# DeltaNet's substitution on VectorE: a reordered mixer in a two-layer kernel on Trainium2

## The chip, the cores and the metric

The kernel runs on one core of one Trainium2 chip. Its engines work side by side, each through its own list of instructions in order: TensorE (PE in the profile) multiplies, VectorE (DVE) and GpSimd (POOL) do elementwise work, ScalarE (ACT) evaluates functions and copies, and SyncE (SP) issues the transfers. An instruction starts when the one ahead of it on its engine is done and the semaphores that it waits for have been raised. The metric is the device time of one execution in microseconds (us), the median of several runs.

## What is computed

Two layers of a backbone run on 384 tokens (128 of a prompt, 256 of a sample) of 1024 features, in float32. Layer 0 mixes the tokens with two recurrences, HGRN2 and a gated DeltaNet, each with four heads and in both directions; layer 1 mixes them with neighbourhood attention; an MLP ends each layer. Only layer 0's mixer is touched. Of the reference that is:

```python
q_a, f_fw, f_bw, i_a, g_a, qkv_b, g_b, a_fw, a_bw, b_fw, b_bw = _split(h @ w_in, _AB_SIZES)
qa = _heads(jax.nn.silu(q_a), H_A) * DK_A ** -0.5
va = _heads(i_a, H_A)
...
qkv = jax.nn.silu(_short_conv(qkv_b, conv_w))
...
# DeltaNet, per chunk of CHUNK tokens and direction:
L = jnp.where(tri, jnp.exp(jnp.where(tri, diff, 0.0)), 0.0)
kb = k * beta[..., None]
A = jnp.where(strict, jnp.einsum('bhntd,bhnsd->bhnts', kb, k) * L, 0.0)
T = jnp.eye(CHUNK) + A
u = triangular_solve(T, v * beta[..., None], lower=True, unit_diagonal=True)
w = triangular_solve(T, kb * jnp.exp(g)[..., None], lower=True, unit_diagonal=True)
```

The shifts, scales and gates of every sub-layer (the modulation) are products of a condition vector with a 1024 x 6144 matrix per layer.

## The kernel before

**Projections.** A weight block of 256 columns arrives in two loads (`raw`, L204, three buffers). ScalarE rounds each to its high half (`whi`, L209), and VectorE, or GpSimd for the blocks named in `ON_POOL`, subtracts to get the low half (`wlo`, L210). Three products of rounded numbers then stand for one in float32. `fm_block` (L645 to L647) makes a block with features on the partitions, 48 matmuls of 384 columns; `tm_half` (L687 to L689) makes the values with tokens on the partitions, 72 matmuls of 256 columns. In the step table f0 to f3 are HGRN's forget gates, q0 and q1 its queries, v0 and v1 its values, c0 to c5 blocks of DeltaNet's queries, keys and values ahead of the convolution (c2 and c3, the keys, are done first, in the part ahead of the table), g0 to g3 output gates, and m the normalised outputs turned into the out-projection's input.

**Evacuations.** `evac_f` (L714, L715) and `evac_q` (L705, L706) make gates and queries, with a sigmoid on ScalarE and an operation on VectorE. `evac_conv` copies a block to `cr` and convolves it on VectorE (L933, L935), and GpSimd multiplies by the sigmoid (L943, L944) ahead of PE's transposes (L949).

**DeltaNet.** A tile is 128 tokens, that is four chunks of 32; there are three tiles, two directions and four heads, 24 matrices of 128 x 128. `gdn_prep` makes the decay `L` (POOL L996) and multiplies the key products by it (L997), and copies each matrix's four diagonal blocks of 32 x 32 to `hyB` (L1000). `gdn_solve` transposes and weights these blocks, sends them through device memory (`s1`, L1038, L1039) so that each of 96 partitions gets one 32 x 32 system (L1043), and inverts all of them by forward substitution: 31 steps of two dependent operations on GpSimd (L1052, L1053). The result goes back through `s2` (L1055, L1057). `gdn_levels` builds inverses of 64 and 128 from them (L1086 and following), with an evacuation times the weights `cd` after each product (L1091, L1120); `gdn_step` runs the recurrence over the tiles.

**HGRN.** `hgrn_tile` multiplies queries by decays (L746, L747), makes the attention's diagonal blocks (PE L745, DVE L748), and then climbs the levels (PE L757, L762; DVE L769, L771, L780).

**Modulation.** `ada_rest` makes what the later sub-layers need, in 12 steps; a step loads two pieces of the matrix (`adr`, two buffers, L323 and L362) and multiplies each by the conditions (PE L326, L367).

**The order.** The table `STEPS` says in which order the parts are written: a letter with a number for a block, h, d and a for some steps of HGRN, DeltaNet and modulation. A scheduler orders each engine's instructions ahead of time, by a simulated timeline with the written order as its priority; on the chip the order is fixed. A table of pairs (`ORDER`) adds constraints: an instruction written inside `behind("x")` is placed no earlier than those marked by the names listed for x. On SP the loads stand in one list with the solve's transfers.

```python
STEPS = """
d f3 f1 f2 d q1 a2 q0 d h a2 h a h c4 h a d h3 d c5 h a2 d h v0 h d h d v1 a d h3
c0 h3 c1 h5 d2 h d2 h d h7 g0 g1 d m g2 g3 a3
"""
ON_POOL = {1: (0, 1), "c5": (0,), "q0": (0,)}
```

## Time and profile before

| | us |
|---|---|
| median of 3 runs | 1136.76 |
| lowest and highest run | 1135.27, 1770.32 |
| the profiled execution | 1139.19 |
| its span in the profile | 1137.3 |
| start: norm, first modulation, first projections (0 to 57) | 57.0 |
| the rest of layer 0's projections and the mixer (57 to 322.6) | 265.6 |
| out-projection, MLP of layer 0, layer 1 (from 322.6) | 814.7 |
| PE busy from 131.0 to 322.6 | 177.3 of 191.6 |

The span is what the profiler saw between the first and the last instruction; the device time of the same execution is 1.9 us longer. The stages are windows of the span: the out-projection's first product begins at 322.58. Rows of a view name the line of the kernel, the engine, the operation, what is written and read (buffer numbers left out), and the shape as partitions x elements.

### The profile page before, as it was taken

Reading aid. Unit: us, or ns where it says so; the run is one execution under the profiler, and the core shown is the slowest. Engines: PE = TensorE matmul, PEld = TensorE weight load, DVE = VectorE, ACT = ScalarE, POOL = GpSimd, SP = SyncE. Lnnn points to the kernel's source line nnn. Section 1 sums busy time; section 2 is a strip of 40 time slices with the busy share of each in tenths; the row PEclk is TensorE's granted clock in tenths of the full one; section 3 lists DMA queues with packets and bytes.
Section 4 is the critical chain, followed back from the end, with each engine's and each line's share of the span. In section 5 each row is a group of like instructions: output and inputs, shape, how many; then the busy total and the mean of one; then the engine's idle time right before and its main releaser. Section 6 shows DMA issues by size and latency. Waiting matters only on the chain.

```text
span 1137.3 us, 17975 instructions
## 1 busy us (share of the span) xinstructions
PE 1081.7 (95%) x6853; PEld 937.8 (82%) x6853; DVE 762.3 (67%) x1188; ACT 485.1 (43%) x874; POOL 277.2 (24%) x295
## 2 busy tenths in 40 slices
PE   6989969999998999999999999999988999999998
PEld 3868857988986898888889788888668889998987
DVE  3678499995467698968887654878748773333333
ACT  4464333342445543433334444656636433333330
POOL 0054894231204011111112252324012011111102
PEclk9989989999998999999999999999989999999999
DMA  8953725333162687766674147566425764433301
GB/s 290 292 168 107 220 79 162 129 108 110 38 218 78 244 275 261 260 202 222 226 248 134 41 101 211 153 185 167 119 74 184 281 203 130 133 126 126 99 38 56
DMA packets 142091, 184.66 MB, mean 162 GB/s; under 512 B 36803, under 2 KB 113685, under 8 KB 142005
## 3 DMA queue, kind: packets, MB, share of 16 engines
q1 hardware_dynamic: 141685, 183.44, 51.0%
q8 instruction: 54, 0.88, 0.3%
q14 instruction: 32, 0.26, 0.1%
q10 hardware_dynamic: 320, 0.07, 0.0%
HBM read 171.53 MB, written 4.61 MB: 155 GB/s over the span
## 4 chain that ended last, share of the span: by engine, by line
PE 74%; DVE 7%; DMA 6%; POOL 6%; issue 2%; SPq 2%; ACT 2%; POOLq 0%; DVEq 0%; ACTq 0%
PE acc L1340 7%; PE acc L1341 7%; PE acc L1342 7%; PE tmp L1355 7%; PE tmp L1356 7%; PE tmp L1354 7%; POOL sm L1053 2%; POOL sm L1052 2%; PE po L1731 2%; DMA ada<-in_ada_w 2%; PE acc L646 2%; PE acc L645 2%; PE acc L647 1%; PE acc L672 1%; PE acc L673 1%
## 5 line engine op out<-in xcount | busy, mean ns | idle before, releaser
L210 DVE TENSOR_TENSOR wlo<-raw,whi 128x1024 fp32r<-128x1024 f32 x192 | 238.0, 1250 | 167.2 <-ACT whi L209 145.5
L209 ACT ACTIVATE whi<-raw 128x1024 fp32r<-128x1024 f32 x198 | 205.9, 1050 | 335.0 <-PE acc L1342 190.6
L1374 POOL TENSOR_TENSOR h<-h 128x384 f32<-128x384 f32 x56 | 69.5, 1242 | 424.9 <-ACT h L1371 423.7
L1341 PE MATMUL acc<-wlo,h 128*128 128x512 f32 x380 | 148.5, 391 | 0.1
L1340 PE MATMUL acc<-whi,h 128*128 128x512 f32 x380 | 146.0, 393 | 0.6 <-issue 0.6
L346 DVE SCALAR_TENSOR_TENSOR adc<-adr,scz,adc 128x1024 f32<-128x1024 f32 x98 | 128.5, 1342 | 10.3 <-DMA adr<-in_ada_w 10.1
L1342 PE MATMUL acc<-whi,h 128*128 128x512 f32 x380 | 121.2, 391 | 0.0
L1340 PEld LDWEIGHTS acc<-whi,h 128*128 128x128 f32 x380 | 71.2, 188 | 20.6 <-ACT whi L209 5.0
L1355 PE MATMUL tmp<-hyA,whi 128*128 128x384 f32 (+1 forms) x256 | 85.1, 333 | 2.2 <-DVE hyA L565 2.2
L1354 PE MATMUL tmp<-hyA,whi 128*128 128x384 f32 (+1 forms) x256 | 84.1, 334 | 3.0 <-DVE hyA L564 3.0
L1354 PE MATMUL tmp<-hyB,whi 128*128 128x384 f32 (+1 forms) x256 | 83.8, 329 | 1.2 <-DVE hyB L564 1.2
L1356 PE MATMUL tmp<-hyA,wlo 128*128 128x384 f32 (+1 forms) x256 | 84.8, 332 | 0.0
L1355 PE MATMUL tmp<-hyB,whi 128*128 128x384 f32 (+1 forms) x256 | 84.0, 329 | 0.7 <-DVE hyB L565 0.7
L1341 PEld LDWEIGHTS acc<-wlo,h 128*128 128x128 f32 x380 | 71.4, 188 | 14.3 <-DVE wlo L210 0.5
L1342 PEld LDWEIGHTS acc<-whi,h 128*128 128x128 f32 x380 | 71.0, 188 | 13.7
L1356 PE MATMUL tmp<-hyB,wlo 128*128 128x384 f32 (+1 forms) x256 | 82.1, 328 | 0.0
L645 PE MATMUL acc<-hyA,whi 128*128 128x384 f32 x208 | 74.1, 356 | 0.0
L646 PE MATMUL acc<-hyA,whi 128*128 128x384 f32 x208 | 71.4, 343 | 0.0
L647 PE MATMUL acc<-hyA,wlo 128*128 128x384 f32 x208 | 71.0, 342 | 0.0
L1375 DVE TENSOR_TENSOR h<-h,h 128x384 fp32r<-128x384 f32 (+2 forms) x72 | 37.8, 526 | 40.6 <-POOL h L1374 39.8
L1354 PEld LDWEIGHTS tmp<-hyA,whi 128*128 128x128 f32 x256 | 48.7, 191 | 4.4 <-ACT km L560 3.4
L1355 PEld LDWEIGHTS tmp<-hyA,whi 128*128 128x128 f32 x256 | 49.3, 192 | 3.3 <-DVE hyA L565 2.4
(454 smaller groups left out, 2357.7 us busy)
## 6 DMA issues: line engine op xcount, KB each, us to landing
raw<-in_w_mlp SPq DMA_DIRECT2D x128, 512.0 KB, 3.8
adr<-in_ada_w SPq DMA_DIRECT2D x80, 512.0 KB, 4.7
raw<-in_w_in_ab SPq DMA_DIRECT2D x34, 512.0 KB, 4.7
ada<-in_ada_w SPq DMA_DIRECT2D x32, 256.0 KB, 5.5
raw<-in_w_qkv_na SPq DMA_DIRECT2D x32, 256.0 KB, 3.8
raw<-in_w_out_ab SPq DMA_DIRECT2D x8, 512.0 KB, 4.5
m<-gs SPq DMA_DIRECT2D x8, 512.0 KB
raw<-in_w_qkv_na SPq DMA_DIRECT2D x8, 512.0 KB
```

The lines of the kernel that those rows point to most:

```text
L209: self.nc.scalar.activation(hi, x, AF.Copy)
L210: (eng or self.nc.vector).tensor_tensor(lo, x, hi.bitcast(F32), op=ALU.subtract)
L346: nc.vector.scalar_tensor_tensor(acc[v], raw, s[v], acc[v], op0=ALU.mult, op1=ALU.add)
L645: nc.tensor.matmul(pg[n], whi(k)[:, c], hhi[:, k], start=(k == 0), stop=False)
L646: nc.tensor.matmul(pg[n], whi(k)[:, c], hlo[:, k], start=False, stop=False)
L647: nc.tensor.matmul(pg[n], wlo(k)[:, c], hhi[:, k], start=False, stop=(k == KT - 1))
L1340: nc.tensor.matmul(pg, shi, w2hi(n)[:, o], start=start, stop=False)
L1341: nc.tensor.matmul(pg, shi, w2lo(n)[:, o], start=False, stop=False)
L1342: nc.tensor.matmul(pg, slo, w2hi(n)[:, o], start=False, stop=last)
L1354: nc.tensor.matmul(pg[n], w1hi(k)[:, c], hhi[:, k, tc_], start=(k == 0), stop=False)
L1355: nc.tensor.matmul(pg[n], w1hi(k)[:, c], hlo[:, k, tc_], start=False, stop=False)
L1356: nc.tensor.matmul(pg[n], w1lo(k)[:, c], hhi[:, k, tc_], start=False, stop=(k == KT - 1))
```

## The change

The substitution goes to VectorE. The 48 systems of one direction lie in partitions 0 to 47 and those of the other in 64 to 111. The diagonal blocks are no longer copied and transposed on the chip: four transfers write them from the matrices to `s1` in pieces of 128 bytes, eight bring them to the partitions; two copies that reverse the order of 48 x 1024 elements stand for the transposition of one direction. After the solve eight transfers write `s2`, four write the inverses straight into the diagonal blocks of the matrices, one brings the other form, which is transposed once. The weights `cd` are multiplied into the matrices when they are made (`weigh`, four operations of 128 x 128 for each), so the levels' evacuations become plain copies on ScalarE; the other scales are renamed to match.

ScalarE also takes the second operation of `evac_f`, a copy in `evac_q` and the convolution's first tap; GpSimd takes the multiplication in `evac_q` and the low halves of v0 and v1, one half of q1 and of c4, and no longer one of c5. The queries' and values' blocks are all written ahead of HGRN's and DeltaNet's steps. HGRN's steps are placed behind the solve, the transposition of its result behind HGRN's query products, some memsets of GpSimd late, and each modulation step marked "!" behind the block ahead of it.

```diff
+    ("step", "!"): ["block"],
+    "hgrn": ["solve"],
+    "solved": ["hq"],
+    "zero": ["q", "lo"],
...
 STEPS = """
-d f3 f1 f2 d q1 a2 q0 d h a2 h a h c4 h a d h3 d c5 h a2 d h v0 h d h d v1 a d h3
-c0 h3 c1 h5 d2 h d2 h d h7 g0 g1 d m g2 g3 a3
+f3 a! f1 f2 a! q1 a! q0 a! v0 a! v1 h3 d2! a! d c4 h a! d h c5 h a! d h3 d h d h a! d2 h3
+c0 a! h3 c1 a! h5 d2 h d2 h d a! h7 g0 g1 d m g2 g3
 """
-ON_POOL = {1: (0, 1), "c5": (0,), "q0": (0,)}
+ON_POOL = {1: (0, 1), "q1": (0,), "q0": (0,), "v0": (0, 1), "v1": (0, 1), "c4": (0,)}
...
-            nc.vector.tensor_mul(self.qa[:, :, h], s, pv)
+            nc.scalar.activation(self.qa[:, :, h], pv, AF.Copy)
+            self.mark["q"] = nc.gpsimd.tensor_tensor(self.qa[:, :, h], self.qa[:, :, h], s, op=ALU.mult)
...
-            nc.vector.tensor_scalar(self.G[:, :, d, h], s, self.lb1[:, h:h + 1], self.lb[:, h:h + 1],
-                                    op0=ALU.mult, op1=ALU.add)
+            nc.scalar.activation(self.G[:, :, d, h], s, AF.Identity, scale=self.lb1[:, h:h + 1], bias=self.lb[:, h:h + 1])
...
-            nc.vector.tensor_scalar(acc, raw[:, 0:386], w(0), None, op0=ALU.mult)
+            nc.scalar.activation(acc, raw[:, 0:386], AF.Copy, scale=w(0))
...
-                nc.vector.tensor_mul(self.NT_[:, t, d], pk, L)
-                for b in range(4):
-                    r = slice(32 * b, 32 * b + 32)
-                    nc.vector.tensor_copy(self.NC[r, d, t], self.NT_[r, t, d, :, r])
+                self.weigh(self.NT_[:, t, d], pk, L, t, d)
+
+    def weigh(self, out, pk, L, t, d):
+        for h in range(4):
+            self.nc.vector.scalar_tensor_tensor(out[:, h], pk[:, h], self.cd[:, t, d, h:h + 1], L[:, h], op0=ALU.mult, op1=ALU.mult)
...
+        for b in range(4):
+            nc.sync.dma_start(s1[rows(b)], self.diagonal(b))
+        for d, x in enumerate((A0, A)):
+            for b in range(4):
+                nc.sync.dma_start(x[part(b, d)], blocks(s1, b, d))
...
+        reverse(A, A0)
+        e, n = nc.vector, 112
         for j in range(31):
             m, w = 31 - j, j + 1
...
+            e.tensor_tensor(t, A[:n, w:, j:j + 1].broadcast_to([n, m, w]), X[:n, j:j + 1, :w].broadcast_to([n, m, w]), op=ALU.mult)
+            self.mark["solve"] = e.tensor_tensor(X[:n, w:, :w], X[:n, w:, :w], t, op=ALU.subtract)
+        reverse(A0, X)
...
+        for d, x in enumerate((A0, X)):
+            for b in range(4):
+                nc.sync.dma_start(blocks(s2, b, d), x[part(b, d)])
+        nc.sync.dma_start(XC, s2)
         for b in range(4):
+            nc.sync.dma_start(self.diagonal(b), s2[rows(b)])
...
-            nc.vector.tensor_mul(pb[T], p[T], cd[T].broadcast_to([32, NT, 4, 32]))
+            nc.scalar.activation(pb[T], p[T], AF.Copy)
...
-            nc.vector.tensor_mul(pb[T, c], p[T, :len(ts)], cd[T, c].broadcast_to([64, len(ts), 4, 64]))
+            nc.scalar.activation(pb[T, c], p[T, :len(ts)], AF.Copy)
...
+        with self.behind("solved"):
+            nc.vector.transpose(self.blocks[:, 1], self.blocks[:, 0])
```

What the scheduler makes of it is seen in each engine's list. First SP, where the results of the solve leave. In the list of before, `sm_139_846` is the solve's result, `s_838` is `s2`, and `raw` and `adr` are weight and modulation loads:

```order
L204 DMA raw_2538<-in_w_in_ab 128x4x256
L362 DMA adr_2283<-in_ada_w 128x1024
L1055 DMA s_838<-sm_139_846 24x32x32 x4
L362 DMA adr_2285<-in_ada_w 128x1024
L388 DMA gs_1936<-ada_1256 2x512 x2
L1057 DMA hyB_645<-s_838 128x768
L204 DMA raw_2540<-in_w_in_ab 128x4x256
```

And of the changed kernel, where `sm_139_826` and `sm_138_825` are the result and its reversed half, `s_832` is `s2`, `m_120_747` the matrices, `raw_1401` belongs to v1, and `raw_1718` and `raw_1720` to c4:

```order
L208 DMA raw_1401<-in_w_in_ab 128x4x256
L208 DMA raw_1718<-in_w_in_ab 128x4x256
L1069 DMA s_832<-sm_139_826 12x32x32 x2
L1069 DMA s_832<-sm_138_825 12x32x32 x4
L1069 DMA s_832<-sm_139_826 12x32x32 x2
L1072 DMA m_120_747<-s_832 32x24x32 x2
L1070 DMA hyB_645<-s_832 128x768
L1072 DMA m_120_747<-s_832 32x24x32 x2
L208 DMA raw_1720<-in_w_in_ab 128x4x256
L329 DMA adr_1391<-in_ada_w 128x1024
L329 DMA adr_1393<-in_ada_w 128x1024
```

The transfers of the solve moved ahead in the list, past ten or more weight loads, and the loads of a fifth modulation step stand behind them.

Second PE, between the values. Before, products of modulation and of HGRN stand among v0's, and loads that came long ahead of the solve's end serve them:

```order
L687 MATMUL acc_2019<-whi_2015,hyA_130 128x256
L326 MATMUL ada_1260<-adr_1926,scz 32x512 x2
L688 MATMUL acc_2019<-whi_2015,hyA_131 128x256
L689 MATMUL acc_2019<-wlo_2016,hyA_130 128x256
L687 MATMUL acc_2019<-whi_2015,hyA_130 128x256
```

In the changed kernel the last products of v0 (`acc_1365`), the fifth modulation step and the first products of v1 (`acc_1411`):

```order
L694 MATMUL acc_1365<-whi_1311,hyA_131 128x256
L695 MATMUL acc_1365<-wlo_1312,hyA_130 128x256
L332 MATMUL ada_994<-adr_1391,scz 32x512 x2
L332 MATMUL ada_994<-adr_1393,scz 32x512 x2
L693 MATMUL acc_1411<-whi_1403,hyA_128 128x256
L694 MATMUL acc_1411<-whi_1403,hyA_129 128x256
```

The values are now whole blocks, and v1 stands behind a modulation step whose loads are those at the end of SP's list above.

Third GpSimd, from the decay's last products on. Before, the steps of the solve begin there, with the products for HGRN's keys (`km`) to follow among them:

```order
L996 TENSOR_TENSOR m_121_750<-m_121_750,tri 128x512 x4
L210 TENSOR_TENSOR wlo_1282<-raw_1277,whi_1281 128x1024
L1046 MEMSET sm_139_846 96x1024
L1047 MEMSET sm_139_846 96x32
L1052 TENSOR_TENSOR sm_140_847<-sm_138_841,sm_139_846 96x31
L1098 MEMSET sm_203_1345 32x12x32
```

In the changed kernel, `wlo_1230` belongs to q0, `wlo_1308` and `wlo_1312` to v0, `wlo_1404` and `wlo_1408` to v1, and L713 are the queries' products:

```order
L214 TENSOR_TENSOR wlo_1230<-raw_1225,whi_1229 128x1024
L745 TENSOR_TENSOR km_1491<-x 128x512
L745 TENSOR_TENSOR km_1514<-x 128x512
L745 TENSOR_TENSOR km_1537<-x 128x512
L214 TENSOR_TENSOR wlo_1308<-raw_1303,whi_1307 128x1024
L214 TENSOR_TENSOR wlo_1312<-raw_1305,whi_1311 128x1024
L713 TENSOR_TENSOR hyB_647<-hyB_647,cv_1209 128x3x128
L713 TENSOR_TENSOR hyB_647<-hyB_647,cv_1213 128x3x128
L214 TENSOR_TENSOR wlo_1404<-raw_1399,whi_1403 128x1024
L713 TENSOR_TENSOR hyB_647<-hyB_647,cv_1287 128x3x128
L214 TENSOR_TENSOR wlo_1408<-raw_1401,whi_1407 128x1024
L713 TENSOR_TENSOR hyB_647<-hyB_647,cv_1291 128x3x128
```

The 62 operations of the solve are gone from GpSimd; on VectorE they now follow one another with a single split (L214) among them, and HGRN's query products (L752, L753) stand right behind.

More of the change, by code (lines that the diff above doesn't have):

```diff
@@ L209, in split @@
         self.nc.scalar.activation(hi, x, AF.Copy)
[L210 removed]
+        ins = (eng or self.nc.vector).tensor_tensor(lo, x, hi.bitcast(F32), op=ALU.subtract)
+        if eng:
+            self.mark["lo"] = ins
     def split_w(self, raws, a, b, ring="", pool=()):
@@ L646, in fm_block @@
                         nc.tensor.matmul(pg[n], whi(k)[:, c], hlo[:, k], start=False, stop=False)
-                        nc.tensor.matmul(pg[n], wlo(k)[:, c], hhi[:, k], start=False, stop=(k == KT - 1))
+                        self.mark["block"] = nc.tensor.matmul(pg[n], wlo(k)[:, c], hhi[:, k], start=False, stop=(k == KT - 1))
         for n in range(2):
@@ L675, in tm_parts, with tm_half @@
         return part
-    def tm_half(self, src, hh, evac):
+    def tm_half(self, src, hh, evac, pool=()):
         nc = self.nc
         hhi, hlo = hh
-        whi, wlo = self.split_w(self.slab(src.rearrange("(k p) n -> p k n", p=P), KT, 256), KT, 256)
+        whi, wlo = self.split_w(self.slab(src.rearrange("(k p) n -> p k n", p=P), KT, 256), KT, 256, pool=pool)
         for t0, n in ((0, 2), (2, 1)):
@@ L688, in tm_half @@
                     nc.tensor.matmul(pg[:, t - t0], hlo[:, k, c], whi(k), start=False, stop=False)
-                    nc.tensor.matmul(pg[:, t - t0], hhi[:, k, c], wlo(k), start=False, stop=(k == KT - 1))
+                    self.mark["block"] = nc.tensor.matmul(pg[:, t - t0], hhi[:, k, c], wlo(k), start=False, stop=(k == KT - 1))
             evac(t0, n, pg)
@@ L794, in hgrn_steps @@
             for x in g:
-                next(x)
+                with self.behind("hgrn"):
+                    next(x)
                 yield
@@ L1022, in gdn_eps, with diagonal @@
         nc.vector.tensor_scalar(self.qe, pq, EPS * EPS * P, None, op0=ALU.add)
+    def diagonal(self, b):
+        r = slice(32 * b, 32 * b + 32)
+        return self.nt[r].rearrange("p d t h c -> p d (t h) c")[:, :, :, r]
     def gdn_solve(self):
         nc = self.nc
-        NC = self.NC
-        f = lambda x: x.rearrange("p d t h c -> p (d t h c)")
-        N2 = self.block(1)
-        nc.vector.transpose(f(N2), f(NC))
-        for d in range(2):
-            nc.vector.tensor_mul(N2[:, d], N2[:, d], self.cd[:, :, d].unsqueeze(3).broadcast_to([P, NT, 4, 32]))
@@ new lines, in gdn_solve @@
+        s1 = self.dp.tile([P, 2, 12, 32], F32, tag="s1", name="s1")
+        s2 = self.dp.tile([P, 2, 12, 32], F32, tag="s2", name="s2")
+        rows = lambda b: slice(32 * b, 32 * b + 32)
+        blocks = lambda s, b, d: s[rows(b), d].rearrange("i m j -> m i j")
+        part = lambda b, d: slice(64 * d + 12 * b, 64 * d + 12 * b + 12)
+        for b in range(4):
+            nc.sync.dma_start(s1[rows(b)], self.diagonal(b))
+        for d, x in enumerate((A0, A)):
+            for b in range(4):
+                nc.sync.dma_start(x[part(b, d)], blocks(s1, b, d))
@@ new lines, in gdn_solve @@
+            self.mark["solve"] = e.tensor_tensor(X[:n, w:, :w], X[:n, w:, :w], t, op=ALU.subtract)
+        reverse(A0, X)
+        XC, XD = (self.blocks[:, j].rearrange("p (d m c) -> p d m c", d=2, c=32) for j in range(2))
+        for d, x in enumerate((A0, X)):
+            for b in range(4):
+                nc.sync.dma_start(blocks(s2, b, d), x[part(b, d)])
+        nc.sync.dma_start(XC, s2)
+        for b in range(4):
+            nc.sync.dma_start(self.diagonal(b), s2[rows(b)])
+        self.Xc = [XD[:, d].rearrange("p (t h) c -> p t h c", t=NT) for d in range(2)]
@@ L1069, in gdn_levels @@
         N = XT = self.NT_
-        cd = self.cd[:, :, d].unsqueeze(3)
         tag = "gd"
-        for b in range(4):
-            r = slice(32 * b, 32 * b + 32)
-            nc.vector.tensor_copy(XT[r, :, d, :, r], self.XTc[d][r])
         first = lambda o, L: slice(o, o + L)
@@ L1097, in gdn_levels @@
         loc = lambda r: slice(r.start - o64, r.stop - o64)
-        nc.gpsimd.memset(X[S, :, :, loc(T)], 0.0)
+        with self.behind("zero"):
+            nc.gpsimd.memset(X[S, :, :, loc(T)], 0.0)
         for r in (S, T):
@@ L1474, in layer0 @@
         for step in STEPS.split():
-            kind, n = step[0], int(step[1:] or 1)
+            kind, n = step[0], int(step[1:].strip("!") or 1)
             if kind in chains:
                 for _ in range(n):
-                    next(chains[kind], None)
+                    with self.behind("step", step[-1]):
+                        next(chains[kind], None)
             elif kind == "f":
```

73 lines of the change are left out of this document (27 added, 46 removed).

## The prediction

> **What bounds the kernel now.** I read the page's engine table and slices first, then the windows over the mixer of layer 0, then what the matmul engine waited for there, then the timelines of the solve.
>
> ```profile
> PE 1081.7 (95%) x6853; PEld 937.8 (82%) x6853; DVE 762.3 (67%) x1188; ACT 485.1 (43%) x874; POOL 277.2 (24%) x295
> 114.00:142.00 28.00, 27.05 (x206) 22.90 (x204) 13.77 (x13) 10.92 (x15) 22.98 (x31) 1.00 0.71 221
> 142.00:171.00 29.00, 20.00 (x311) 17.13 (x310) 28.96 (x34) 9.12 (x15) 27.16 (x27) 0.88 0.26 85
> 131.10:322.60 191.50, 177.22 (x1942) 160.12 (x1941) 152.99 (x245) 71.79 (x156) 79.66 (x90) 0.97 0.36 111
> PE tmp L949 <- POOL cv L943: 5.4, 2, 3.1
> PE hg L757 <- DVE hyB L748: 2.8, 1, 2.8
> PE hg L757 <- DVE hyB L771: 2.4, 2, 1.4
> ```
>
> A window row gives its length, then the busy time of PE, PEld, DVE, ACT and POOL with their counts, the granted clock and the DMA share. TensorE is busy 95% of the span, so a change of the other engines can win only where PE idles or runs slowly, or lose by making PE wait. The changed code lies between about 75 and 322.6 us, where the out-projection begins. From 131.1 on, PE idles 191.5 - 177.2 = 14.3 us; 9.0 of that lies between 142 and 171, where VectorE is busy all the time and GpSimd 27.2 of 29. The waits name the convolution's products on GpSimd, queued behind the solve, and HGRN's levels on VectorE. That idle time, with the slow clock behind it, is what the change can win.
>
> ```profile
> 117.38 0.25 POOL L1052 TENSOR_TENSOR sm<-sm,sm 96x31 f32<-96x31 f32 x1 [5.71 <-DMA sm<-s]
> 180.30 0.58 POOL L1053 TENSOR_TENSOR sm<-sm,sm 96x31 f32<-96x31 f32 x1
> 108.10 0.33 SPq L1039 DMA_DIRECT2D s<-g  x1
> 112.95 2.10 SPq L1043 DMA_DIRECT2D sm<-s  x4
> 180.91 2.06 SPq L1055 DMA_DIRECT2D s<-sm  x4
> 185.59 0.34 SPq L1057 DMA_DIRECT2D hyB<-s  x1
> 131.06 0.62 PE L326 MATMUL ada<-adr,scz 128*32 128x512 f32 x2
> 122.28 0.44 PE L645 MATMUL acc<-hyA,whi 128*128 128x384 f32 x1
> 322.58 0.48 PE L672 MATMUL acc<-whi,hyB 128*128 128x512 f32 x1
> ```
>
> The solve holds GpSimd from 117.4 to 180.9, with other work between. Its results are back after a hop of about 9 us, yet PE has the projections of c4, c5 and the values to do meanwhile, so no wait names the solve itself. A projection block takes 131.06 - 122.28 = 8.8 us. Blocks and modulation steps end at 131.1, and the rest of the mixer takes 191.5 us more.
>
> **The solve on VectorE.** 62 operations of 31 to 256 elements, 10,912 elements in all.
>
> ```profile
> 91.61 0.18 DVE L971 TENSOR_TENSOR cd<-beta,kr 128x24 f32<-128x24 f32 x1
> 117.69 1.23 DVE L210 TENSOR_TENSOR wlo<-raw,whi 128x1024 fp32r<-128x1024 f32 x1 [5.16 <-ACT whi L209]
> L997 DVE TENSOR_TENSOR m<-hg,m 128x512 f32<-128x512 f32 x6 | 4.1, 685 | 0.1
> L1000 DVE COPY hyB<-m 32x128 f32<-32x128 f32 x24 | 7.3, 304 | 0.4
> L1167 DVE SCALAR_TENSOR_TENSOR sm<-sm,eg,gd 128x128 f32<-128x128 f32 x8 | 2.2, 342 | 0.0
> ```
>
> Two rows fix the price: 0.18 us for 24 elements and 1.23 for 1024 make (1.23 - 0.18)/1000 = 1.05 ns an element and 0.155 fixed. A dependent step adds about 0.045 (from L971's start to L972's below it is 0.22 us, against 0.18 busy). So 62 x 0.2 + 10,912 x 1.05 ns = 23.9 us, plus one split of 1.2 that stands in the middle. On GpSimd it was 63.5.
>
> Ahead of it, the 24 weighted products at 0.34 (L1167) replace 6 at 0.69 and 24 copies at 0.30: 8.2 for 11.4 us, and two transposes and two products go. I put the last product at 98. The first hop out stands on SP's queue behind a weight load whose buffer waits for GpSimd's split, so I put its four issues at 99.5 to 101.6. From L1039's issue to the first L1043 passes 4.85 us; eight issues in place of four, 0.52 each by L1043 and L1055, take 4.2, and from the last issue to the first operation 2.3 passed before. The solve starts at 101.1 + 4.85 + 4.2 + 2.3 = about 112, for 117.4.
>
> **Contention.** Beside the solve, GpSimd now has the low halves of v0 and v1 (q0's comes just ahead), three products that make HGRN's keys (`km`), and four query products: about 17 us.
>
> ```profile
> 91.83 1.29 DVE L972 TENSOR_TENSOR cs<-cd,eg 128x24 f32<-128x24 f32 x1
> 91.80 3.74 POOL L996 TENSOR_TENSOR m<-m,tri 128x512 f32<-128x512 f32 x3
> 134.81 3.44 DVE L747 TENSOR_TENSOR hq<-hyB,m 128x512 f32<-128x512 f32 x1
> 135.33 2.38 POOL L210 TENSOR_TENSOR wlo<-raw,whi 128x1024 fp32r<-128x1024 f32 x1
> L944 POOL TENSOR_TENSOR m<-cv,cv 128x256 f32<-128x256 f32 x8 | 7.4, 927 | 0.0
> L739 POOL TENSOR_TENSOR km<-x 128x512 f32<-128x512 f32 x3 | 3.8, 1274 | 0.0
> L769 DVE TENSOR_TENSOR x<-x,m 128x512 f32<-128x512 f32 x21 | 18.2, 878 | 0.1
> ```
>
> The 17 us: four splits at 2.38, three products for keys at 1.27, and four products of 384 elements at about 0.95 (an estimate, near L944's 256 elements and under the 512 of L739) make 17.1. L972, as small as L971, took 1.29 in place of 0.18, as long as one of the GpSimd products beside it; L747 took 3.44, and 2.38 of it lies under one GpSimd split. Against that L769, much of which ran beside GpSimd's small solve steps, is at 0.88 on average, some quarter above the 0.69 that L997 takes for as many. Every operation of the solve waits for the one before it, so a stall cannot be made up. The lower end is 0, the upper 17; the splits are of the form that held up L747 wholly, some of the 17 us may lie ahead of the solve, and I take 10. The solve then ends at Ts = 112 + 23.9 + 1.2 + 10 = 147; by the ends 137 and 154.
> The Trainium skill, page "SBUF — State Buffer", section on who interferes with whom, has a VectorE operation with two SBUF inputs and a GpSimd operation exclude each other for a whole instruction. L972's 1.29 agrees with that, L769's 0.88 less plainly; the fourth rival is this case.
>
> **The queue behind the solve.** On SP, behind the solve's eight writes (L1069 of the new kernel, which wait for its end), the four back into the triangles and the one into `hyB`, now stands the modulation load `adr_1391`. On PE its products stand between v0 and v1, and v1, HGRN and DeltaNet's levels stand behind them.
>
> ```profile
> 115.15 0.98 SPq L323 DMA_DIRECT2D adr<-in_ada_w  x2
> 88.70 0.74 PE L645 MATMUL acc<-hyA,whi 128*128 128x384 f32 x1
> 119.96 1.05 PE L326 MATMUL ada<-adr,scz 128*32 128x512 f32 x4 [0.67 <-DMA adr<-in_ada_w]
> 121.29 1.05 PE L326 MATMUL ada<-adr,scz 128*32 128x512 f32 x4 [0.28 <-DMA adr<-in_ada_w]
> 184.93 0.38 PE L687 MATMUL acc<-whi,hyA 128*128 128x256 f32 x1
> 189.22 0.28 PE L689 MATMUL acc<-wlo,hyA 128*128 128x256 f32 x1
> 78.50:88.90 10.40, 9.76 (x32) 5.39 (x32) 5.37 (x10) 8.33 (x22) 4.48 (x6) 0.58 0.49 168
> 366.00:370.50 4.50, 4.39 (x20) 4.39 (x21) 1.96 (x5) 1.45 (x3) 0.55 (x1) 0.50 0.39 118
> ```
>
> After Ts come eight issues at 0.52 (4.2), their landing (L1055's last issue at about 182.4, L1057 at 185.6 with two other issues between: 2.5), five issues more (1.8) and the two loads' own (0.9): the second load is issued at Ts + 9.4. The rows of `adr` give 119.96 - 115.15 = 4.8 and, for the second, issued some 0.5 later, 5.6; I take 5.0. So the step's products start at Ts + 14.4 = 161.4 and take 1.0.
>
> PE gets there much earlier. f1 starts at 88.7 as before, f1, f2, q1 and q0 take 4 x 8.8, four modulation steps some 1.0 each, and v0 36 matmuls in 4.57 us twice (the two rows of values: 184.93 to 189.50), 9.1: v0 ends at 137. PE stands still for about 24 us; the ends of the stall give 14 to 31. After that v1 takes 9.1, plus a slow clock: the two last rows, windows just behind idle stretches, show 10.4 us at 0.58 and 4.5 us at 0.50, a loss of 4.4 and 2.2; I take 3.
> On this the Trainium skill, page "TensorE: Matmul & The Clock Gate", part 1, has about 3.4 us of half rate after an idle stretch, which would lose 1.7; the two stretches here are longer, and the measurement decides.
>
> **The rest of the mixer.** What PE did after 131.1 was 191.5 us. The values in it go: 144 matmuls at 4.57/36 are 18.3, and 15 of them at half rate 1.4, so 19.7. The same seven modulation steps are left. I drop all 14.3 us of idle time: GpSimd no longer holds the convolution's products back, and HGRN's inputs are done while PE stands. Left: 157.5 (a few us of slow clock stay in it, as an allowance for waits that I cannot see).
>
> End of the mixer: Ts + 14.4 + 1.0 + 9.1 + 3 + 157.5 = Ts + 185.0 = 332, against 322.6: 9.4 us later. Layer 0's MLP and layer 1 are untouched. The span 1137.3 becomes 1146.7; the profiled execution took 1139.19, 2.4 more than the median of 1136.76, so I add the difference to the median: 1146.
>
> **The smaller edits, at nothing.**
>
> ```profile
> L1010 DVE TENSOR_TENSOR m<-gd,m 128x512 f32<-128x512 f32 x6 | 3.8, 683 | 2.6 <-PE gd L1008 2.6
> L1074 DVE COPY m<-hyB 32x384 f32<-32x384 f32 x8 | 4.3, 539 | 0.1
> L1120 DVE TENSOR_TENSOR sm<-gd,cd 64x512 f32<-64x512 f32 (+1 forms) x4 | 2.2, 556 | 2.0 <-PE gd L1118 1.9
> L1091 DVE TENSOR_TENSOR g<-gd,cd 32x384 f32<-32x384 f32 x4 | 2.2, 554 | 0.1
> ```
>
> The two pb evacuations (L1091, L1120) go to ScalarE, 4.4 us off VectorE, and so do the convolution's first tap and evac_f: ScalarE is busy 71.8 of 191.5. The attention's weights cost VectorE 8.2 for 3.8; L1074's eight copies (4.3) go, so VectorE comes out about even and stays below PE: 153.0 less the query products and splits moved ahead or to GpSimd. If that cover fails it is the second rival. HGRN behind the solve, and the memsets late, lie inside PE's stall. Where they lie ahead of f1 they win nothing either: I keep its start at 88.7.
>
> **The rivals.**
> First, no stall: if the load lands before v0 ends (Ts under 122, hence a solve of under 10 us, or another issue order), v1 ends at 137 + 1 + 9.1 = 147.1, the mixer at 304.6, and the time is 1118.8. For it: PE's 14.3 idle us do go and the solve is much shorter. Against it: the queue's order is fixed.
> Second, on the other side: VectorE keeps PE waiting after v1 as it did, because the attention's weights, the levels and HGRN's tiles now fall together with nothing but GpSimd to share them. If PE loses the 14.3 us again, the time is 1146 + 14.3 = 1160.3. For it: VectorE's 28.96 of 29 from 142 to 171, where PE lost 9.0. Against it: GpSimd's solve, which slowed VectorE there, is gone. It decides if VectorE is busy more than 0.97 in the 60 us after v1.
> Third, the change does next to nothing: GpSimd and VectorE interleave, the stall is 0 to 3 us, PE's pause of 14 to 17 us eats the idle time won. Ts = 137 to 140, time 1136 to 1139. L769's row speaks for it, L972's against.
> Fourth, the solve waits out all of GpSimd's 17.1 us, as L747 waited out a split: Ts = 154, and the time is 1146 + 7 = 1153. For it L972 and L747, against it L769.
>
> **How the numbers follow.** Chances: the forecast (1139 to 1151) 0.40, no stall 0.14, VectorE-bound 0.18, next to nothing 0.14, all of the stall 0.14. The predicted time is the forecast's 1146. The range leaves out part of the first rival and the upper part of the second, 0.1 on either side: 1121 to 1160. Beyond 2%, about what a measurement of this kernel can tell from no change, means under 1114 or over 1159.5: faster takes 0.05 (no stall and less slow clock), slower 0.13 (two thirds of the second rival, and a little of the fourth).
>
> **What would show it.** Right: a PE wait of 14 to 31 us for `adr` between v0 and v1, a half-rate clock behind it, the solve from about 112 to 147 with operations of 0.2 to 0.45 us and some stretched to over 1 beside GpSimd's splits, no wait of over 1 us for the convolution's GpSimd products. Wrong: the load issued ahead of the solve's writes, a solve of 25 us beside busy GpSimd, or waits for VectorE of over 10 us after v1.

## The result and the profile after

The changed kernel takes 1148.29 us (median of 4 runs, 1146.67 to 1151.33) for 1136.01 of the kernel before beside it: a ratio of 1.0115 [1.0093, 1.0137]. One of the four runs of the kernel before was a slow one, 1770.32 us, and is not in the ratio; without it that median is 1135.27, and the change is 13.0 us slower. That is clear of the noise (the interval is 0.2% to either side), though under the 2% that the prediction took as the least that can be told. The profiled execution took 1148.93, its span is 1147.2, 9.9 longer than before.

The engine table of the page after the change:

```profile
PE 1073.2 (94%) x6853; PEld 933.8 (81%) x6853; DVE 747.4 (65%) x1214; ACT 500.8 (44%) x906; POOL 251.0 (22%) x243
```

VectorE and GpSimd have less to do and ScalarE more, as the change means it; TensorE stays the engine that sets the time. What PE waited for between 74 us and the out-projection (total, times, longest):

```profile
PE ada L332 <- DMA adr<-in_ada_w: 27.1, 1, 27.1
PE tmp L955 <- ACT cv L960: 4.5, 1, 4.5
```

One wait of 27.1 us stands where many small ones stood; those for the convolution on GpSimd and for the levels on VectorE are gone. Windows over v0, the stall with the modulation step, v1, the rest of the mixer up to the out-projection, and one inside that rest:

```profile
129.76:138.66 8.90, 8.90 (x76) 8.69 (x72) 8.49 (x13) 2.41 (x4) 4.69 (x4) 1.00 0.01 2
138.66:168.97 30.31, 3.19 (x9) 0.38 (x9) 17.84 (x42) 1.33 (x2) 8.69 (x6) 0.55 0.45 110
168.97:177.97 9.00, 9.00 (x81) 8.87 (x83) 0.38 (x1) 1.69 (x3) 0.00 (x0) 0.99 0.69 227
177.97:335.79 157.82, 154.59 (x1796) 140.30 (x1797) 120.04 (x228) 73.33 (x164) 36.23 (x39) 0.99 0.36 116
177.97:237.97 60.00, 60.00 (x955) 49.28 (x955) 45.94 (x73) 31.58 (x59) 9.27 (x9) 1.00 0.47 150
```

v0 and v1 are whole blocks of 9 us at full clock. Behind v1, PE idles only 3.2 us up to the out-projection, where it idled 14.3 from 131.1 on before; that is what the change gives. In the 30.3 us between, PE works 3.2. The rows of SP, which issues the transfers, show what it waited for:

```profile
120.03 2.47 SPq L208 DMA_DIRECT2D raw<-in_w_in_ab  x2
151.01 4.51 SPq L1069 DMA_DIRECT2D s<-sm  x8
...
157.96 1.24 SPq L1072 DMA_DIRECT2D m<-s  x2
159.25 0.64 SPq L208 DMA_DIRECT2D raw<-in_w_in_ab  x1
159.93 1.32 SPq L329 DMA_DIRECT2D adr<-in_ada_w  x2
```

From 122.5 to 151.0 SP issues nothing: the next in its list is the solve's result, whose end it awaits. The load of the modulation step, which depends on nothing of this, leaves at 159.9. The eight writes left behind 23 loads of `raw` and 8 of `adr`, where the writes of before left behind 29 and 17. The step's products on PE, the first of v1's, and the first of the out-projection:

```profile
165.78 3.25 PE L332 MATMUL ada<-adr,scz 128*32 128x512 f32 x8 [27.13 <-DMA adr<-in_ada_w]
168.97 0.50 PE L693 MATMUL acc<-whi,hyA 128*128 128x256 f32 x1
...
335.79 0.48 PE L678 MATMUL acc<-whi,hyB 128*128 128x512 f32 x1
```

The eight products take 3.2 us where such a step took 1.05 before. The granted clock is 0.50 from 165.78 to 169.23, 3.45 us, and full from there on, so the clock's cost ends with the first products of v1.
The Trainium skill, page "TensorE: Matmul & The Clock Gate", part 1, has about 3.4 us of half rate after an idle stretch; this trace agrees, with 3.45 us, while in the experiment "c4 ahead" below half rate lasts 34 us, with short waits in it.

The solve itself, on VectorE, and what GpSimd does beside it:

```profile
114.05 0.54 DVE L1062 TENSOR_TENSOR sm<-sm,sm 112x31 f32<-112x31 f32 x1 [1.91 <-DMA sm<-s]
...
117.43 2.42 DVE L1062 TENSOR_TENSOR sm<-sm,sm 112x87 f32<-112x87 f32 x1
119.88 2.32 DVE L1063 TENSOR_TENSOR sm<-sm,sm 112x87 f32<-112x87 f32 x1
...
127.17 2.45 DVE L1062 TENSOR_TENSOR sm<-sm,sm 112x207 f32<-112x207 f32 x1
129.66 1.07 DVE L1063 TENSOR_TENSOR sm<-sm,sm 112x207 f32<-112x207 f32 x1
130.76 2.47 DVE L1062 TENSOR_TENSOR sm<-sm,sm 112x220 f32<-112x220 f32 x1
...
149.76 0.25 DVE L1063 TENSOR_TENSOR sm<-sm,sm 112x87 f32<-112x87 f32 x1
...
150.79 0.19 DVE L1063 TENSOR_TENSOR sm<-sm,sm 112x31 f32<-112x31 f32 x1
```

```profile
116.54 5.55 POOL L214 TENSOR_TENSOR wlo<-raw,whi 128x1024 fp32r<-128x1024 f32 x2 [0.74 <-ACT whi L213]
122.06 2.03 POOL L713 TENSOR_TENSOR hyB<-hyB,cv 128x384 f32<-128x384 f32 x2
126.94 2.46 POOL L214 TENSOR_TENSOR wlo<-raw,whi 128x1024 fp32r<-128x1024 f32 x1 [2.85 <-ACT whi L213]
129.36 1.13 POOL L713 TENSOR_TENSOR hyB<-hyB,cv 128x384 f32<-128x384 f32 x1
130.44 2.54 POOL L214 TENSOR_TENSOR wlo<-raw,whi 128x1024 fp32r<-128x1024 f32 x1
```

The sizes of the substitution rise and fall again, so each operation of the first half has an undisturbed twin in the second: 87 elements take 2.42 beside GpSimd and 0.25 alone. Measured against their twins, the four low halves hold the solve up by 2.17 + 2.07 + 2.07 + 2.08 = 8.4 us, the products for the keys by 1.4 and the four products of the queries by 2.8 (1.07 for 0.38, for instance): together 12.6 of the 36.9 from 114.05 to 150.98.

### The profile page after: what moved, and what is told of

It is laid out like the page before. It is cut to its first block, busy times and chain, and to the rows that moved or that the text cites. A ratio compares the mean times of both kernels' runs of the same rounds, so it can differ in the third digit from the quotient of the medians.

```text
span 1147.2 us, 17999 instructions
## 1 busy us (share of the span) xinstructions
PE 1073.2 (94%) x6853; PEld 933.8 (81%) x6853; DVE 747.4 (65%) x1214; ACT 500.8 (44%) x906; POOL 251.0 (22%) x243
## 4 chain that ended last, share of the span: by engine, by line
PE 76%; DVE 11%; DMA 6%; SPq 3%; ACT 2%; issue 2%; POOL 1%; DVEq 0%; POOLq 0%; ACTq 0%
PE acc L1351 7%; PE acc L1352 7%; PE tmp L1366 7%; PE acc L1353 7%; PE tmp L1367 7%; PE tmp L1365 7%; DMA ada<-in_ada_w 2%; PE acc L651 2%; PE acc L652 2%; PE acc L679 2%; PE acc L653 2%; PE acc L678 2%; PE acc L680 2%; DVE sm L1062 2%; PE po L1743 2%
## 5 line engine op out<-in xcount | busy, mean ns | idle before, releaser
L214 DVE TENSOR_TENSOR wlo<-raw,whi 128x1024 fp32r<-128x1024 f32 (+1 forms) x187 | 230.1, 1240 | 177.4 <-ACT whi L213 165.7
L1352 PEld LDWEIGHTS acc<-wlo,h 128*128 128x128 f32 x380 | 71.4, 188 | 14.4 <-DVE wlo L214 0.7
L651 PE MATMUL acc<-hyA,whi 128*128 128x384 f32 x208 | 72.2, 349 | 1.1 <-ACT hyB L712 1.1
L652 PE MATMUL acc<-hyA,whi 128*128 128x384 f32 x208 | 70.6, 340 | 0.0
```

What stands on the lines that cost most here:

```text
L214: ins = (eng or self.nc.vector).tensor_tensor(lo, x, hi.bitcast(F32), op=ALU.subtract)
L651: nc.tensor.matmul(pg[n], whi(k)[:, c], hhi[:, k], start=(k == 0), stop=False)
L652: nc.tensor.matmul(pg[n], whi(k)[:, c], hlo[:, k], start=False, stop=False)
L1352: nc.tensor.matmul(pg, shi, w2lo(n)[:, o], start=False, stop=False)
```

## The experiments

All were timed in 3 or 5 rounds, beside the kernel before on the same chip (medians 1137.99, 1135.68 and 1136.41 us in the three groups). The last column is where the out-projection starts in the profile.

| experiment | group | median us | ratio to before, 95% | out-projection |
|---|---|---|---|---|
| the change | – | 1148.29 | 1.0115 [1.0093, 1.0137] | 335.79 |
| step behind v1 | 1 | 1141.75 | 1.0050 [1.0033, 1.0066] | 327.31 |
| low halves by memset | 1 | 1140.96 | 1.0032 [1.0010, 1.0054] | 326.62 |
| loads ahead | 1 | 1131.96 | 0.9958 [0.9936, 0.9979] | 313.88 |
| loads ahead, again | 3 | 1132.93 | 0.9953 [0.9934, 0.9972] | 314.09 |
| old order | 1 | 1158.73 | 1.0199 [1.0169, 1.0230] | 337.16 |
| old order, marked | 2 | 1156.59 | 1.0192 [1.0174, 1.0210] | 335.76 |
| taps and gates back | 2 | 1148.66 | 1.0123 [1.0105, 1.0140] | 335.12 |
| c4 ahead | 2 | 1136.36 | 1.0008 [0.9990, 1.0026] | 325.26 |
| and values on VectorE | 2 | 1137.33 | 1.0009 [0.9993, 1.0025] | 326.10 |
| step behind c4 | 3 | 1129.43 | 0.9940 [0.9921, 0.9959] | 320.15 |
| c4 and c5 ahead | 3 | 1134.37 | 0.9980 [0.9965, 0.9996] | 319.10 |

The last column is of one profiled execution each, and from there to the span's end it is another 805 to 823 us. Executions of one kernel differ by several us (the profiled one of "c4 ahead" took 1132.00 for a median of 1136.36, that of "step behind c4" 1133.76 for 1129.43), and some products stand on another side of that point (4229 to 4267 of TensorE's are behind it). So small differences in this column count for little, and the medians decide.

### The low halves by memset

The four low halves of v0 and v1 that fall beside the solve become memsets of the same size on the same engine. The values then lack the product with the low half of their weights.

```diff
-        ins = (eng or self.nc.vector).tensor_tensor(lo, x, hi.bitcast(F32), op=ALU.subtract)
+        ins = self.nc.gpsimd.memset(lo.bitcast(F32), 0.0) if eng and self.blank else (eng or self.nc.vector).tensor_tensor(lo, x, hi.bitcast(F32), op=ALU.subtract)
```

> The changed kernel with GpSimd's four subtractions for the low halves of v0 and v1 replaced by memsets of the same tiles, in the same places of its list (the values then lack their low product). Theory (a VectorE operation of the solve stands still while a GpSimd operation reads SBUF beside it): the four stretched steps of 2.3 to 2.5 us become 0.25 to 0.4, the solve takes 28.5 in place of 36.9 us, the wait for adr falls from 27 to about 19, and the time falls by 8 to about 1140. Rival (any GpSimd instruction, or the wait for another engine, stretches them): the solve stays at 35 us or more, and the time within 3 us of 1148.

The groups of the solve's operations on VectorE, first with the changed kernel (count, busy, mean ns, then the idle time before them):

```profile
L1062 DVE TENSOR_TENSOR sm<-sm,sm 112x31 f32<-112x31 f32 (+15 forms) x31 | 18.0, 580 | 2.9 <-DMA sm<-s 1.9
L1063 DVE TENSOR_TENSOR sm<-sm,sm 112x31 f32<-112x31 f32 (+15 forms) x31 | 15.8, 511 | 1.1
```

And with the memsets:

```profile
L1063 DVE TENSOR_TENSOR sm<-sm,sm 112x31 f32<-112x31 f32 (+15 forms) x31 | 13.4, 431 | 1.1
L1062 DVE TENSOR_TENSOR sm<-sm,sm 112x31 f32<-112x31 f32 (+15 forms) x31 | 12.4, 401 | 2.8 <-DMA sm<-s 1.8
```

33.8 us become 25.8, so 8.0 of the 8.4 go. One of the memsets on GpSimd, and an operation of the solve on VectorE that ran beside it:

```profile
117.05 0.95 POOL L214 MEMSET wlo<- 128x1024 f32 x1 [1.11 <-PE acc L653]
```

```profile
117.24 0.28 DVE L1062 TENSOR_TENSOR sm<-sm,sm 112x112 f32<-112x112 f32 x1
```

An operation of 112 elements takes 0.28 beside a memset, the same as undisturbed. The solve lasts 28.9 us, PE waits 18.9 for `adr` in place of 27.1, the out-projection starts 9.2 earlier, and the time falls from 1148.29 to 1140.96, as expected. It is GpSimd's operations that read SBUF which hold VectorE, not GpSimd's being busy, and in this order, where PE waits for what stands behind the solve, a stall of the solve passes to the end in full.
The Trainium skill, page "SBUF — State Buffer", section on who interferes with whom, says that a VectorE operation with two SBUF inputs contends with a GpSimd one that reads SBUF and not with one that only writes; the rows of this pair agree, with 2.4 against 0.28 us. The prediction gave this rule without the condition that GpSimd's operation reads SBUF; all that it counted do, and the memset is the case that it left out.

### The step behind v1

v1 moves ahead of the modulation step whose load is late, so that PE has another 9 us to do.

```diff
-    "hgrn": ["solve"],
+    "hgrn": ["solve", "block"],
...
-f3 a! f1 f2 a! q1 a! q0 a! v0 a! v1 h3 d2! ...
+f3 a! f1 f2 a! q1 a! q0 a! v0 v1 a! h3 d2! ...
```

> The changed kernel with the fifth modulation step written behind v1, and HGRN's first operations held behind v1 too; the loads stay behind the solve's transfers on SP. Theory (the load is late because of its place in SP's queue, and everything on TensorE behind its products waits): v1 now fills 9 us of the wait, the wait for adr shrinks from 27 to about 18 us and stands behind v1, the time falls by 9 to about 1139. Rival 1 (TensorE would wait for the solve's result anyway): the same 27 us are waited, named after something else, and the time stays within 3 us of 1148. Rival 2 (VectorE is what bounds the rest): the stall shrinks but the rest of the mixer grows by as much, time within 3 us of 1148.

The out-projection starts 8.5 us earlier and the median falls by 6.5, where 9 were expected. But the wait that is left, 19.1 us, stands inside v1 and is put down to ScalarE's evacuation of the accumulator (L1476). ScalarE's timeline shows why that was late:

```profile
163.74 1.06 ACT L213 ACTIVATE whi<-raw 128x1024 fp32r<-128x1024 f32 x1 [23.94 <-DMA raw<-in_w_in_ab]
164.70 0.85 ACT L1476 ACTIVATE hyB<-acc 128x256 f32<-128x256 f32 x2
```

Ahead of the evacuation ScalarE's order has the split of a weight whose load, too, stands on SP behind the solve's result. So the step's load was only the first that PE met; the cause is the queue, and a wait named for ScalarE was a transfer's.

### Loads ahead

The writes of the solve's result become a step "s" of their own in the list, behind v0 and the step's loads, and every write of `s2` is ordered behind a load of `adr`.

```diff
+    "out": ["adr"],
...
-f3 a! f1 f2 a! q1 a! q0 a! v0 a! v1 h3 d2! ...
+f3 a! f1 f2 a! q1 a! q0 a! v0 a! s v1 h3 d2! ...
...
+    def solve_out(self):
...
+                with self.behind("out"):
+                    nc.sync.dma_start(blocks(s2, b, d), x[part(b, d)])
```

> The changed kernel with the solve's transfers written out behind the fifth modulation step's loads, so that these two loads stand ahead of them in SP's list; the step's place on TensorE, between v0 and v1, is kept. Theory (the place in SP's queue is the cause): no wait for that step, v1 follows v0 at once, and TensorE then waits some 10 us in all for the solve's end and for the next step's load; the time falls by 15 to 20, to 1128 to 1134. Rival 1 (TensorE waits for the solve anyway): 20 us or more are waited at HGRN's or the levels' first products, time 1142 or more. Rival 2 (VectorE bounds the rest): the wait goes and comes back in pieces after v1, time above 1138.

```profile
127.09 0.82 SPq L330 DMA_DIRECT2D adr<-in_ada_w  x2
...
151.96 2.08 SPq L1077 DMA_DIRECT2D s<-sm  x4
154.14 1.02 SPq L330 DMA_DIRECT2D adr<-in_ada_w  x2
155.25 2.17 SPq L1077 DMA_DIRECT2D s<-sm  x4
```

These rows of SP's timeline show the step's load now at 127.1, ahead of the transfers. PE's wait of 27 us for it is gone, v1 follows v0 at once, and the next load of the kind, caught between the two halves of the transfers, makes PE wait 12.1 us at the sixth step (158.54). The time is 1131.96, 0.4% faster than the kernel before, and the same again in a second pair:

> The kernel with the fifth step's loads ahead of the solve's transfers once more, on the chip of the two others: 0.4% under the kernel before, as measured (0.9936 to 0.9979).

1132.93, ratio 0.9953 [0.9934, 0.9972]. So the whole change is worth a little once the first load that PE meets is no longer queued behind the solve's result: the two medians are 16 us apart, and only that order differs. What the solve's move to VectorE is worth by itself is not shown by this.

### The old order, and the old order marked

Old table of steps, old sharing with GpSimd, and no order between the solve, HGRN and the transposition; the substitution stays on VectorE with its operands.

```diff
-    "hgrn": ["solve"],
-    "solved": ["hq"],
+    "hgrn": [],
+    "solved": [],
...
-f3 a! f1 f2 a! q1 a! q0 a! v0 a! v1 h3 d2! ...
+d f3 f1 f2 d q1 a2 q0 d h a2 h a h c4 h a d h3 d c5 h a2 d h v0 h d h d v1 a d h3
...
-ON_POOL = {1: (0, 1), "q1": (0,), "q0": (0,), "v0": (0, 1), "v1": (0, 1), "c4": (0,)}
+ON_POOL = {1: (0, 1), "c5": (0,), "q0": (0,), "v0": (), "v1": ()}
```

> The changed kernel with the step table, the list of GpSimd's splits and the order of HGRN behind the solve as they were before; the solve on VectorE, the folded weights and ScalarE's share stay. Theory (the solve's move is good by itself, and the new order costs the time): no long wait for adr, the waits of before for GpSimd's convolution products (5.4 us) go, and the time is 1126 to 1133, under that of before. Rival (the solve on VectorE is too long for that place, VectorE being busy all the time from 142 to 171): TensorE waits for VectorE instead, time 1137 or more.

This expectation failed: it is the slowest of all, at 1158.73. PE's largest waits, with VectorE's row in the middle of the solve behind them:

```profile
PE ada L332 <- DMA adr<-in_ada_w: 15.0, 6, 4.2
PE ada L373 <- DMA adr<-in_ada_w: 6.4, 4, 2.5
```

```profile
142.60 0.68 DVE L389 TENSOR_TENSOR ada<-ada,ada 64x512 f32<-64x512 f32 x1 [6.01 <-PE ada L332]
```

Without the mark that ties a modulation step to a block, the steps' products bunch up between 118.7 and 154.4 and eight of those ten waits for a load lie there; an operation of theirs stands in VectorE's order among the solve's and holds it for 6 us. The second kernel keeps the old table with the mark on each "a":

```diff
-d f3 f1 f2 d q1 a2 q0 d h a2 h a h c4 ...
+d f3 f1 f2 d q1 a2! q0 d h a2! h a! h c4 ...
```

> The kernel with the old step table (solve on VectorE), with each modulation step marked to stand behind the block ahead of it, so that the eight steps no longer bunch ahead of q0. Theory (in that table the order puts DeltaNet's first levels, L1094, among q0's products, and they are not ready before about 161 us): TensorE now waits some 30 us for hyB at L1094 in place of 15 and 6 us for loads, and the time is 1155 to 1168. Rival (the bunched steps and their loads are themselves the cost): the waits go, and the time is 1128 to 1138.

```profile
PE gd L1094 <- DVE hyB L1211: 14.6, 1, 14.6
PE ada L332 <- DMA adr<-in_ada_w: 11.4, 1, 11.4
```

The bunch is gone and the time hardly changes (1156.59, inside the 1155 to 1168 that were expected). PE now waits 14.6 us for the solve's result itself, since the old table has the levels' first products (L1094) that early, and 11.4 for a load that SP issued behind 16.6 us of weight loads waiting for their buffers. One wait of some 30 us for the result was expected; half of it came, and the other wait is again one for a load. So the reordering does its part: with the substitution on VectorE, the old table and sharing stand at 1.02 against before, the new ones at 1.0115.

### Taps and gates back

The convolution's first tap and the second operation of `evac_f` go back to VectorE.

```diff
-            nc.scalar.activation(self.G[:, :, d, h], s, AF.Identity, scale=self.lb1[:, h:h + 1], bias=self.lb[:, h:h + 1])
+            nc.vector.tensor_scalar(self.G[:, :, d, h], s, self.lb1[:, h:h + 1], self.lb[:, h:h + 1], op0=ALU.mult, op1=ALU.add)
...
-            nc.scalar.activation(acc, raw[:, 0:386], AF.Copy, scale=w(0))
+            nc.vector.tensor_scalar(acc, raw[:, 0:386], w(0), None, op0=ALU.mult)
```

> The changed kernel with the convolution's first tap and the second operation of evac_f back on VectorE. Theory (VectorE's work up to the solve's end lies on the path through the load's wait): the gates' eight operations of 0.67 and the taps' 0.58 put the solve's end 4 to 7 us later, the wait for adr grows by as much, time 1152 to 1156. Rival (these edits cost and bring nothing, as the prediction had them): time within 2 us of 1148.

A loss of a few us was expected, and there is none: 1148.66, a ratio of 1.0123 that overlaps the change's. The solve even starts 4.8 us earlier (109.28). It lasts 38.9 us for 36.9, with the products for the keys now wholly beside it, and ends 2.8 earlier (148.21). PE's waits:

```profile
PE ada L332 <- DMA adr<-in_ada_w: 25.4, 1, 25.4
PE acc L651 <- ACT hyB L712: 3.3, 1, 3.3
```

The wait for the load is 1.7 shorter, another one 2.2 longer (1.1 in the changed kernel). So the out-projection starts 0.7 us earlier. Moving these operations is worth nothing either way that shows, as the prediction had it.

### c4 ahead, and the values on VectorE

From "loads ahead": c4 stands ahead of "s" too, with both low halves on GpSimd, the transfers stand behind all loads written ahead of "s", and later loads behind the transfers. HGRN's steps are held behind the block ahead of them as well as behind the solve.

```diff
-    "hgrn": ["solve"],
+    "hgrn": ["solve", "block"],
+    "out": ["adr", "raw"],
+    "late": ["outs", "xc"],
...
-... v0 a! v1 h3 d2! a! d c4 h a! ...
+... v0 a! v1 c4 s h3 d2! a! d h a! ...
...
-... "v0": (0, 1), "v1": (0, 1), "c4": (0,)}
+... "v0": (0, 1), "v1": (0, 1), "c4": (0, 1)}
```

> From the kernel whose fifth step's loads stand ahead of the solve's transfers: the block c4 is written ahead of them too and follows v1 on TensorE, both its low halves are made on GpSimd, and every later load is held behind the solve's transfers. Theory (TensorE needs independent work until the solve's result is back, and any load behind the transfers comes 12 us after the solve's end): c4's 8.4 us fill most of the 12 us that were still waited there, and the time falls by 4 to 9 below that kernel, to 1123 to 1129. Rival (GpSimd's two further splits stretch the solve by up to 4 us, and what follows c4 waits for c5's loads behind the transfers): the wait only moves behind c4, time 1130 or more.

1136.36, no better than before and worse than "loads ahead": the time is the rival's. The sixth step no longer waits 12 us, but PE waits in pieces, of which the longest is:

```profile
PE hg L755 <- DVE hyB L758: 5.2, 1, 5.2
```

Six splits on GpSimd stand beside the solve, for five in "loads ahead"; it ends at 154.8 for 151.9, and HGRN's steps, which stand behind it on VectorE, come later. Yet the waits are no longer in all: from 130 to 200 us PE is idle for 11.4 us, in "loads ahead" for 13.3. What is lost beyond them shows in the clock. The same window in "loads ahead" and here:

```profile
159.00:193.00 34.00, 32.88 (x478) 27.64 (x475) 23.34 (x34) 16.92 (x31) 7.14 (x8) 0.94 0.72 201
159.00:193.00 34.00, 26.39 (x306) 18.27 (x307) 20.10 (x30) 11.13 (x17) 6.48 (x8) 0.50 0.66 193
```

Here PE is busy for 26.4 of the 34 us, at half its clock all the while. At full clock that work would take about 13 us less (an estimate, half of the 26.4); in "loads ahead" the clock of 0.94 costs about 2 (0.06 of 34). What keeps the clock low was not tried; short waits and small products alternate there. The next kernel takes the values' low halves off GpSimd as well:

```diff
-ON_POOL = {... "v0": (0, 1), "v1": (0, 1), "c4": (0, 1)}
+ON_POOL = {... "v0": (), "v1": (), "c4": (0, 1)}
```

> As the one with c4 ahead, with the four low halves of v0 and v1 made on VectorE, between steps of the solve. Theory (a GpSimd split stretches the solve by about 2.1 us, on VectorE it costs 1.23): the solve ends 3 us earlier, and the time falls by 0 to 3 against the one with c4 ahead. Rival (VectorE's own list holds the splits up, so that v0 or v1 wait for them): TensorE waits ahead of the values, and the time is 2 us or more longer.

The solve ends 4.5 us earlier (150.24), and the time is the same, 1137.33; the two are not told apart. What is won there is lost ahead of v0:

```profile
129.20 3.19 PE L336 MATMUL ada<-adr,scz 128*32 128x512 f32 x8 [2.81 <-DMA adr<-in_ada_w]
```

PE waits 2.8 us for a modulation step that it did not wait for in "c4 ahead", takes 3.2 us for it in place of 1.1, and begins v0 at 132.3 in place of 127.5. The step's loads leave at 124.6 in place of 119.6, behind a weight load that leaves when VectorE's split of 122.88 is done, at 124.1. So VectorE's list holds PE up ahead of the values, as the rival had it, by way of a load. The clock of 0.50 is here too, from 168 to 193.

### The step behind c4, and c4 and c5 ahead

The first keeps "loads ahead" and puts c4 ahead of the sixth modulation step; the second takes "c4 ahead" and puts c5 ahead of "s" as well, its low halves on GpSimd.

```diff
-... v0 a! v1 h3 d2! a! d c4 h a! ...
+... v0 a! s v1 h3 c4 d2! a! d h a! ...
```

> From the kernel whose fifth step's loads stand ahead of the solve's transfers: only the order of two things is changed further, c4 is written ahead of the sixth modulation step, so that its products stand on TensorE ahead of that step's, whose loads come behind the solve. Theory (what is still waited there, 12 us, is that step's load): half of c4 fills it, the other half waits for its split behind the solve on VectorE until about 157; 5 to 8 us are won, time 6 us under that kernel, 1123 to 1128. Rival (nothing is ready before the solve's result is back, whatever the order): the wait goes to c4's second half or to L1102, time within 2 us of that kernel.

1129.43 is the lowest median of all, but above the 1123 to 1128 that were expected, and its interval overlaps that of "loads ahead": the two are not told apart. The profile shows no gain either: its two waits are 13.1 us, the one in "loads ahead, again" was 12.4. The wait moved once more, to c4:

```profile
PE acc L654 <- DVE wlo L215: 8.3, 1, 8.3
PE acc L652 <- ACT hyB L1484: 4.8, 1, 4.8
```

```profile
165.72 1.06 ACT L214 ACTIVATE whi<-raw 128x1024 fp32r<-128x1024 f32 x1 [18.33 <-DMA raw<-in_w_in_ab]
```

The 8.3 us are a low half of c4 that VectorE makes only behind the solve and HGRN's query products (158.14 to 160.49). The 4.8 are, as with the step behind v1, an evacuation of v1 (L1484) that stands on ScalarE behind the split of a weight whose load is queued behind the transfers; ScalarE stands 18.3 us for that load.

```diff
-... v0 a! v1 h3 d2! a! d c4 h a! d h c5 h ...
+... v0 a! v1 c4 c5 s h3 d2! a! d h a! d h h ...
```

> As the kernel with c4 ahead, with c5 and its loads ahead of the solve's transfers too, four splits of c4 and c5 on GpSimd. Theory: TensorE has 17 us of blocks behind v1, until about 163, when the levels can start, and the pieces of wait there (12 us) go; against it GpSimd's two further splits stretch the solve by 4 us. Time 1124 to 1132. Rival (the convolutions on VectorE come behind the solve and the levels start later, so that the end of DeltaNet moves out): 1136 or more.

1134.37, between the 1132 expected at most and the rival's 1136, with eight splits on GpSimd beside the solve, for the change's four, and a solve of 45 us (114.82 to 159.98). PE's largest wait, and the rows behind it:

```profile
PE tmp L959 <- POOL cv L953: 7.5, 1, 7.5
```

```profile
164.12 2.57 DVE L945 SCALAR_TENSOR_TENSOR cv<-cr,prm,cv 128x386 f32<-128x386 f32 x4
167.39 0.45 POOL L953 TENSOR_TENSOR cv<-cv,cv 128x128 f32<-128x128 f32 x1 [7.11 <-ACT cv L947]
```

GpSimd, which the wait names, had been idle for 7.1 us. It waited for ScalarE's sigmoid, and that for the convolution on VectorE, which stands behind the longer solve and HGRN's query products: the mechanism is the rival's. In the orders tried behind "loads ahead", PE kept standing idle for some 7 to 13 us from 130 to 200, in one wait or another.

## Why the prediction was right

**The place and the mechanism.** A PE wait of 14 to 31 us for `adr` between v0 and v1 was forecast, at about 24, and 27.1 came (138.66 to 165.78, forecast 137 to 161.4). That the queue makes it is shown from two sides: putting the load ahead removes the wait and 16 us, and shortening the solve by 8 us shortens the wait by 8.

**The sum, term by term.** The solve ended at 150.98, forecast 147: it began 2.1 late (114.05 for 112), most of it behind the last of the eight issues (4.2 us to the first operation, where 2.3 were taken), and it lasted 36.9 for 35.1. Of the second, the stall was 12.6 for 10; the split in the middle took 1.05 for 1.2 and the rest 23.3 for 23.9, since operations of 256 elements follow each other in 0.45 us where my price gives 0.47. From the solve's end to the step's products it was 14.8 for 14.4. The step, v1 and the slow clock took 12.2 for 13.1: about 2.1 were lost where I took 3 from windows behind other idle stretches, and 3.45 us at 0.50 account for 1.7 of them. What follows v1 took 157.8 for 157.5, by two errors that cancel: I had PE busy all the time, with a few us of slow clock as an allowance for waits; it was busy 154.6 and idle 3.2. These errors add to +3.8: the out-projection began at 335.79, forecast 332.

**A term that was set to nothing.** The span is 9.9 us longer and not 13.2, so 3.3 seem regained behind the mixer, where I had taken everything as untouched. The sums of four windows from the out-projection to the end, before and after:

```profile
sum 814.42, PE 787.76 PEld 688.94 DVE 531.25 ACT 350.37 POOL 153.62; mean PE 196.94 PEld 172.23 DVE 132.81 ACT 87.59 POOL 38.41
```

```profile
sum 811.21, PE 786.64 PEld 687.60 DVE 529.38 ACT 349.91 POOL 153.32; mean PE 196.66 PEld 171.90 DVE 132.34 ACT 87.48 POOL 38.33
```

Of the 3.2, PE was idle 26.7 us before and 24.6 after, and busy 1.1 less. The runs do not bear this out as an effect of the change: the time rose by 13.0 us, as much as the out-projection moved. The profiled execution of before stood 3.9 us above 1135.27, the median above, that of the change 0.6, and two profiles of "loads ahead" differ by 4.4 in span (1127.4 and 1131.8) behind the same start of the out-projection. So taking this part as untouched holds as far as the runs show.

**What was luck.** The change was forecast at +9.4 us and came to +13.0, which is 3.6 too low, about the 3.8 of the sum. That 1146 lies only 2.3 below 1148.29 is partly luck: its base, 1136.76, was 1.5 above the 1135.27 of the runs beside the change.

**The stall.** The row chosen for it, a split that held up VectorE for its whole length, was right in kind: each split stretched one operation by 2.1 us, and all four fell beside the solve. The size was between my 10 and the upper end of 17.1: the splits gave 8.4 of their 9.5, the queries' products 2.8 of 3.8, and the products for the keys 1.4 of 3.8, because they began 2.2 us ahead of the solve. An operation that takes 2.42 beside a split would have taken 0.25 anyway, so only the difference is lost; with that and the early keys, the solve stays below the sum of GpSimd's times, and the fourth rival's 17.1 were too high.

**The rivals.** No stall fell with the queue's order. VectorE-bound fell by its own condition: in the 60 us behind v1 VectorE is busy 45.9, or 0.77, and PE does not idle. Next to nothing, with a stall of 0 to 3 us, fell with the 12.6 us of stretched operations. The smaller edits at nothing held where it was tried (taps and gates); the weights' products and the evacuations were not tried alone.

**What was not settled.** The substitution on GpSimd under the new order was not tried, so how much of the result belongs to the engine alone is open.
